# Hand-written engine programs with staging freed by each cast, a GpSimd relay of casts to TensorE's loop, and PSUM copies of four banks

## Chip, cores and metric

One Trainium2 chip, one core. The metric is the device time of one execution in microseconds (us). One run is one execution. "Span" is the time from the first to the last instruction of the profiled execution; the device time is 1.7 to 2.2 us longer.

Some terms. A semaphore is a counter on which an engine can wait. Each transfer adds 16 to its semaphore, in the transfers over 128 partitions one for each of the 16 DMA engines as it finishes its share; the last of the 16 is the landing. The *lag* below is the time from the median to the last of these increments, so how far the slowest DMA engine is behind. PSUM is the memory into which TensorE writes its sums; a group of two banks is 128x1024 float32 here. The granted clock is the share of its full clock that TensorE was given.

## The reference

```python
batch, m, k, n = 16, 512, 768, 1024
x: (16, 768, 512) float32      y: (16, 768, 1024) float32
out = np.einsum('bkm,bkn->bmn', x, y)          # (16, 512, 1024) float32
```

Each batch reads 1.57 MB of x and 3.15 MB of y and writes 2.10 MB. All 16 batches make 109.05 MB, and the kernel before and after move exactly these bytes.

## The kernel before

Four engine programs in one block. SyncE loads x and y into two staging buffers each, and stores. VectorE casts to bf16. TensorE runs 96 matmuls per loop round (two batches), 8 rounds. ScalarE copies PSUM to one of five output buffers, two banks at a time.

```python
LAG = 4; NO = 5                                    # stores lag 4 batches; 5 output buffers
# (cut: allocation of xs, ys, xb, yb (2 each), ob (5), ps (4 groups of 2 banks), semaphores)
@block.sync
def _(sync):
    def store(b):
        sync.wait_ge(outs, b + 1)
        sync.dma_start(o_v[b], ob[b % NO][:]).then_inc(so[b % NO], 16)
    for b in range(B):
        i = b % 2
        if b >= 2:
            sync.wait_ge(cast, b - 1)              # all casts of batch b-2
        sync.dma_start(xs[i][:], x_v[b]).then_inc(sx[i], 16)
        sync.dma_start(ys[i][:], y_v[b]).then_inc(sy[i], 16)
        if b >= LAG:
            store(b - LAG)
    for b in range(B - LAG, B):
        store(b)
    # (cut: wait for all stores)

@block.vector
def _(vector):
    for b in range(B):
        # (cut: i, ks; wait for TensorE's batch b-2, for x)
        nc.vector.tensor_copy(xb[i][:], xs[i][:]).then_inc(ready, 1)
        # (cut: wait for y)
        for h in range(2):                         # y in two halves of K
            nc.vector.tensor_copy(yb[i][:, ks], ys[i][:, ks]).then_inc(ready, 1)
        vector.drain().then_inc(cast, 1)

@block.scalar
def _(scalar):
    nc.scalar.nop().then_inc(room, MT)
    for b in range(B):
        for mo in range(MT):                       # 4 groups of 2 banks
            # (cut: waits for the output buffer and for TensorE's group)
            nc.scalar.copy(ob[b % NO][:, mo]..., ps[mo][:]).then_inc(room, 1)
        scalar.drain().then_inc(outs, 1)
```

Of the kernel before, what the change touches and what calls it, by code (L numbers as in the profile page):

```python
# [1 line left out]

_os.environ.setdefault("NEURON_RT_ULTRASERVER_MODE", "4")

# [1 line left out]

# [4 lines left out]


@with_exitstack
def kernel(
    ctx: ExitStack,
    tc: tile.TileContext,
    x: bass.AP,
    y: bass.AP,
    out: bass.AP,
):  # L20
    nc = tc.nc
    P = 128
    FP32 = mybir.dt.float32
    BF16 = mybir.dt.bfloat16

    B, K, M = x.shape
    _, _, N = y.shape
    KT = K // P
    MT = M // P
    NF = 512  # L30
    NT = N // NF



    x_v = x.rearrange("b (p ko) m -> b p ko m", ko=KT)
    y_v = y.rearrange("b (p ko) n -> b p ko n", ko=KT)
    o_v = out.rearrange("b (p mo) n -> b p mo n", mo=MT)

    LAG = 4
    NO = 5  # L40
    KH = KT // 2
    GP = NT * NF

    ctx.enter_context(tc.tile_critical())  # L44
    ec = ctx.enter_context
    xs = [ec(nc.sbuf_tensor(f"xs{i}", [P, KT, M], FP32)) for i in range(2)]
    ys = [ec(nc.sbuf_tensor(f"ys{i}", [P, KT, N], FP32)) for i in range(2)]
    xb = [ec(nc.sbuf_tensor(f"xb{i}", [P, KT, M], BF16)) for i in range(2)]
    yb = [ec(nc.sbuf_tensor(f"yb{i}", [P, KT, N], BF16)) for i in range(2)]
    ob = [ec(nc.sbuf_tensor(f"ob{i}", [P, MT, N], FP32)) for i in range(NO)]  # L50
    ps = [ec(nc.psum_tensor(f"ps{i}", [P, NT, NF], FP32)) for i in range(MT)]
    sx = [ec(nc.semaphore(f"sx{i}")) for i in range(2)]
    sy = [ec(nc.semaphore(f"sy{i}")) for i in range(2)]
    so = [ec(nc.semaphore(f"so{i}")) for i in range(NO)]
    cast = ec(nc.semaphore("cast"))
    ready = ec(nc.semaphore("ready"))
    room = ec(nc.semaphore("room"))
    groups = ec(nc.semaphore("groups"))
    outs = ec(nc.semaphore("outs"))
    block = ec(nc.Block())  # L60

    @block.sync
    def _(sync):
        def store(b):
            sync.wait_ge(outs, b + 1)
            sync.dma_start(o_v[b], ob[b % NO][:]).then_inc(so[b % NO], 16)

        for b in range(B):
            i = b % 2
            if b >= 2:  # L70
                sync.wait_ge(cast, b - 1)
            sync.dma_start(xs[i][:], x_v[b]).then_inc(sx[i], 16)
            sync.dma_start(ys[i][:], y_v[b]).then_inc(sy[i], 16)
            if b >= LAG:
                store(b - LAG)
        for b in range(B - LAG, B):
            store(b)
        for i in range(NO):
            sync.wait_ge(so[i], 16 * len(range(i, B, NO)))

    @block.vector
    def _(vector):
        for b in range(B):
            i = b % 2
            n = 16 * (b // 2 + 1)
            if b >= 2:
                vector.wait_ge(groups, MT * (b - 1))
            vector.wait_ge(sx[i], n)
            nc.vector.tensor_copy(xb[i][:], xs[i][:]).then_inc(ready, 1)  # L89
            vector.wait_ge(sy[i], n)  # L90
            for h in range(2):
                ks = slice(h * KH, (h + 1) * KH)
                nc.vector.tensor_copy(yb[i][:, ks], ys[i][:, ks]).then_inc(ready, 1)  # L93
            vector.drain().then_inc(cast, 1)

    def batch(tensor, i, first):
        x_w = xb[i][:].rearrange("p k (j mo) -> p k mo j", mo=MT)
        tensor.wait_ge(ready, 2).then_inc(ready, -2)
        for mo in range(MT):
            tensor.wait_ge(room, 1).then_inc(room, -1)  # L100
            for nt in range(NT):
                for kt in range(KT):
                    if mo == 0 and nt == 0 and kt == KH:
                        tensor.wait_ge(ready, 1).then_inc(ready, -1)
                    mm = nc.tensor.matmul(  # L105
                        ps[mo][:, nt], x_w[:, kt, mo],
                        yb[i][:, kt, nt * NF:(nt + 1) * NF],
                        start=(kt == 0), stop=(kt == KT - 1))
            mm.then_inc(groups, 1)

    @block.tensor
    def _(tensor):
        with tensor.Fori(0, B // 2):
            batch(tensor, 0, False)
            batch(tensor, 1, False)

    @block.scalar
    def _(scalar):
        nc.scalar.nop().then_inc(room, MT)
        for b in range(B):  # L120
            for mo in range(MT):
                if mo == 0 and b >= NO:
                    scalar.wait_ge(so[b % NO], 16 * (b // NO))
                scalar.wait_ge(groups, MT * b + mo + 1)
                nc.scalar.copy(ob[b % NO][:, mo].rearrange("p (t f) -> p t f", f=NF),  # L125
                               ps[mo][:]).then_inc(room, 1)
            scalar.drain().then_inc(outs, 1)


# [1 line left out]
_INS = ['x', 'y']  # L131
_OUTS = [((16, 512, 1024), 'float32')]


# [23 lines left out]
```

## Time and profile before

| | before |
|---|---|
| device time, median | 262.99 us (262.69 to 263.14, 3 runs) |
| span | 261.2 us |
| data queue, share of 16 DMA engines | 98.1% |
| TensorE, VectorE, ScalarE busy | 72%, 32%, 25% |
| last copy out of PSUM ends / store 15 issued / last byte confirmed | 250.72 / 250.78 / 259.79 us |

The first question to such a table is which row leaves no room. No compute engine does; the transfers do. The second question is whether that holds at the very end, because there a store has to wait for the last copy. The lines are in the prediction.

### The profile page before, as it was taken

What the parts mean: (1) busy time and instruction counts of PE and PEld (TensorE: products, weight loads), DVE (VectorE), ACT (ScalarE), POOL (GpSimd) and SP (SyncE); (2) the same over time, 40 slices, a digit from 0 to 9 for tenths busy, and PEclk for the clock granted to TensorE, in tenths of its full rate; (3) what the DMA queues carried; (4) which work ended last, traced back from release to release, by engine and by line L of the source; (5) the groups of instructions that cost most, each with busy time, mean ns of one, the idle gap of its engine ahead of it and who ended that gap; (6) DMA issues with size and microseconds to landing.
All of it is one profiled execution on the core that took longest, in us unless ns stands there. A gap on an engine that the chain in (4) does not pass through costs nothing. (4 is left out here: it accounts for less than half of the span.)

```text
span 261.2 us, 1938 instructions
## 1 busy us (share of the span) xinstructions
PE 188.0 (72%) x768; PEld 87.1 (33%) x768; DVE 83.0 (32%) x48; ACT 66.1 (25%) x65; POOL 0.2 (0%) x4
## 2 busy tenths in 40 slices
PE   0039999998948949398595997939678394896920
PEld 0014555443513515144152342514334142342500
DVE  0261734435223252322524214252132523225000
ACT  1003343433331314114032140412314033131410
POOL 0000000000000000000000000000000000000000
PEclk9999999999986999979798697997999899797995
DMA  7999999999999999999999999999999999999993
GB/s 265 431 425 427 438 411 453 425 386 418 446 420 439 420 430 446 415 441 420 439 437 412 447 423 440 415 432 442 423 434 420 435 433 423 440 433 421 434 421 141
DMA packets 6915, 109.09 MB, mean 418 GB/s; under 512 B 768, under 2 KB 768, under 8 KB 768
## 3 DMA queue, kind: packets, MB, share of 16 engines
q1 hardware_dynamic: 6912, 109.05, 98.1%
q8 instruction: 1, 0.02, 0.0%
q14 instruction: 2, 0.02, 0.0%
HBM read 75.50 MB, written 33.55 MB: 417 GB/s over the span
## 5 line engine op out<-in xcount | busy, mean ns | idle before, releaser
L105 PE MATMUL ps<-yb,xb 128*128 128x512 bf16 x768 | 188.0, 406 | 61.6 <-PEq L100 55.9
L105 PEld LDWEIGHTS ps<-yb,xb 128*128 128x128 bf16 x768 | 87.1, 116 | 162.1 <-issue 96.7
L125 ACT COPY ob<-ps 128x1024 f32<-128x1024 f32 x64 | 64.9, 1013 | 183.6 <-PE ps L105 183.6
L93 DVE CAST yb<-ys 128x3072 bf16<-128x3072 f32 x32 | 54.9, 1757 | 88.4 <-DMA ys<-in_y_dram 88.4
L89 DVE CAST xb<-xs 128x3072 bf16<-128x3072 f32 x16 | 28.2, 1760 | 67.5 <-DMA xs<-in_x_dram 66.8
L125 ACT ACT_TABLE_LOAD x1 | 1.3, 1283 | 1.0 <-SPq L44 1.0
L142 POOL MEMSET const-uint8-127<- 128x1 uint8 x1 | 0.1, 102 | 0.0
L142 POOL MEMSET const-bfloat16-1.0<- 128x1 bf16 x1 | 0.1, 101 | 0.0
L142 POOL MEMSET const-float32-0.0<- 128x1 f32 x1 | 0.1, 98 | 0.2 <-issue 0.2
L142 POOL MEMSET const-float32-1.0<- 128x1 f32 x1 | 0.1, 98 | 0.0
## 6 DMA issues: line engine op xcount, KB each, us to landing
ys<-in_y_dram SPq DMA_DIRECT2D x16, 3072.0 KB, 27.7
out_dram<-ob SPq DMA_DIRECT2D x16, 2048.0 KB, 32.1
xs<-in_x_dram SPq DMA_DIRECT2D x16, 1536.0 KB, 20.8
```

The costliest lines, as they stand in the source:

```text
L89: nc.vector.tensor_copy(xb[i][:], xs[i][:]).then_inc(ready, 1)
L93: nc.vector.tensor_copy(yb[i][:, ks], ys[i][:, ks]).then_inc(ready, 1)
L105: mm = nc.tensor.matmul(ps[mo][:, nt], x_w[:, kt, mo], yb[i][:, kt, nt * NF:(nt + 1) * NF], start=(kt == 0), stop=(kt == KT - 1))
L125: nc.scalar.copy(ob[b % NO][:, mo].rearrange("p (t f) -> p t f", f=NF), ps[mo][:]).then_inc(room, 1)
L142: nc = _bacc.Bacc("TRN2", target_bir_lowering=False, num_devices=1)
```

## The change

Its intent: issue each load as soon as its own staging buffer is free, halve the ScalarE instructions, cast y in one instruction where TensorE has time, let stores 0 to 13 wait for TensorE's next batch, and drop the block with its entry and exit. VectorE now counts all casts in one semaphore `cast`; GpSimd waits on fixed values of it and feeds `ready`, which TensorE's loop decrements.

```diff
-    ps = [... [P, NT, NF] ... for i in range(MT)]          # 4 groups of 2 banks
+    ps = [... [P, HB, NT, NF] ... for i in range(2)]       # 2 groups of 4 banks
-    block = ec(nc.Block())                                 # (all programs now stand without it)
+    def parts(b):
+        return 2 if b in (0, 1, 2, 14, 15) else 1
     def store(b):
-            sync.wait_ge(outs, b + 1)
+        if b < B - 2:
+            nc.sync.wait_ge(groups, 2 * (b + 2))            # TensorE's batch b+1 done
+        else:
+            nc.sync.wait_ge(outs, b - (B - 3))
     for b in range(B):
         if b >= 2:
-                sync.wait_ge(cast, b - 1)
+            nc.sync.wait_ge(cast, nx[b - 2])                # x cast of b-2
         dma_start(xs[i][:], x_v[b])
+        if b >= 2:
+            nc.sync.wait_ge(cast, nx[b - 2] + parts(b - 2)) # last y cast of b-2
         dma_start(ys[i][:], y_v[b])
-            for h in range(2):                              # y cast in halves, then a drain
+        for h in range(parts(b)):                           # one y cast in batches 3 to 13
+    for b in range(B):
+        nc.gpsimd.wait_ge(cast, nx[b]).then_inc(ready, 1)
+        for h in range(parts(b)):
+            nc.gpsimd.wait_ge(cast, nx[b] + h + 1).then_inc(ready, 2 // parts(b))
     # ScalarE: 2 copies of 128x2048 per batch instead of 4 of 128x1024; drain only in batch 14
     # (cut: TensorE's loop, same 96 matmuls, now room/groups per 4 banks)
```

More of the change, by code (lines that the diff above doesn't have):

```diff
@@ L10 @@
 from concourse._compat import with_exitstack
+from concourse.ordered_engine_set import OrderedEngineSet
 @with_exitstack
@@ L41 @@
     KH = KT // 2
-    GP = NT * NF
     ctx.enter_context(tc.tile_critical())
@@ L50 @@
     ob = [ec(nc.sbuf_tensor(f"ob{i}", [P, MT, N], FP32)) for i in range(NO)]
-    ps = [ec(nc.psum_tensor(f"ps{i}", [P, NT, NF], FP32)) for i in range(MT)]
+    HB = MT // 2
+    ps = [ec(nc.psum_tensor(f"ps{i}", [P, HB, NT, NF], FP32)) for i in range(2)]
     sx = [ec(nc.semaphore(f"sx{i}")) for i in range(2)]
@@ L59 @@
     outs = ec(nc.semaphore("outs"))
-    block = ec(nc.Block())
-    @block.sync
-    def _(sync):
-        def store(b):
-            sync.wait_ge(outs, b + 1)
-            sync.dma_start(o_v[b], ob[b % NO][:]).then_inc(so[b % NO], 16)
-        for b in range(B):
-            i = b % 2
-            if b >= 2:
-                sync.wait_ge(cast, b - 1)
-            sync.dma_start(xs[i][:], x_v[b]).then_inc(sx[i], 16)
-            sync.dma_start(ys[i][:], y_v[b]).then_inc(sy[i], 16)
-            if b >= LAG:
-                store(b - LAG)
-        for b in range(B - LAG, B):
-            store(b)
-        for i in range(NO):
-            sync.wait_ge(so[i], 16 * len(range(i, B, NO)))
@@ L81, in _ @@
-    @block.vector
-    def _(vector):
-        for b in range(B):
-            i = b % 2
-            n = 16 * (b // 2 + 1)
-            if b >= 2:
-                vector.wait_ge(groups, MT * (b - 1))
-            vector.wait_ge(sx[i], n)
-            nc.vector.tensor_copy(xb[i][:], xs[i][:]).then_inc(ready, 1)
-            vector.wait_ge(sy[i], n)
-            for h in range(2):
-                ks = slice(h * KH, (h + 1) * KH)
-                nc.vector.tensor_copy(yb[i][:, ks], ys[i][:, ks]).then_inc(ready, 1)
-            vector.drain().then_inc(cast, 1)
@@ L96, in batch @@
-    def batch(tensor, i, first):
-        x_w = xb[i][:].rearrange("p k (j mo) -> p k mo j", mo=MT)
-        tensor.wait_ge(ready, 2).then_inc(ready, -2)
-        for mo in range(MT):
-            tensor.wait_ge(room, 1).then_inc(room, -1)
-            for nt in range(NT):
-                for kt in range(KT):
-                    if mo == 0 and nt == 0 and kt == KH:
-                        tensor.wait_ge(ready, 1).then_inc(ready, -1)
-                    mm = nc.tensor.matmul(
-                        ps[mo][:, nt], x_w[:, kt, mo],
-                        yb[i][:, kt, nt * NF:(nt + 1) * NF],
-                        start=(kt == 0), stop=(kt == KT - 1))
-            mm.then_inc(groups, 1)
@@ L111, in _ @@
-    @block.tensor
-    def _(tensor):
-        with tensor.Fori(0, B // 2):
-            batch(tensor, 0, False)
-            batch(tensor, 1, False)
-    @block.scalar
-    def _(scalar):
-        nc.scalar.nop().then_inc(room, MT)
-        for b in range(B):
-            for mo in range(MT):
-                if mo == 0 and b >= NO:
-                    scalar.wait_ge(so[b % NO], 16 * (b // NO))
-                scalar.wait_ge(groups, MT * b + mo + 1)
-                nc.scalar.copy(ob[b % NO][:, mo].rearrange("p (t f) -> p t f", f=NF),
-                               ps[mo][:]).then_inc(room, 1)
-            scalar.drain().then_inc(outs, 1)
+    def parts(b):
+        return 2 if b in (0, 1, 2, 14, 15) else 1
@@ new lines, with store @@
+    nx = [sum(1 + parts(a) for a in range(b)) + 1 for b in range(B)]
+    def store(b):
+        if b < B - 2:
+            nc.sync.wait_ge(groups, 2 * (b + 2))
+        else:
+            nc.sync.wait_ge(outs, b - (B - 3))
+        nc.sync.dma_start(o_v[b], ob[b % NO][:]).then_inc(so[b % NO], 16)
+    for b in range(B):
+        i = b % 2
+        if b >= 2:
+            nc.sync.wait_ge(cast, nx[b - 2])
+        nc.sync.dma_start(xs[i][:], x_v[b]).then_inc(sx[i], 16)
+        if b >= 2:
+            nc.sync.wait_ge(cast, nx[b - 2] + parts(b - 2))
+        nc.sync.dma_start(ys[i][:], y_v[b]).then_inc(sy[i], 16)
+        if b >= LAG:
+            store(b - LAG)
@@ new lines @@
+    for b in range(B - LAG, B):
+        store(b)
+    for b in range(B):
+        i = b % 2
+        n = 16 * (b // 2 + 1)
+        if b >= 2:
+            nc.vector.wait_ge(groups, 2 * (b - 1))
+        nc.vector.wait_ge(sx[i], n)
+        nc.vector.tensor_copy(xb[i][:], xs[i][:]).then_inc(cast, 1)
+        nc.vector.wait_ge(sy[i], n)
+        for h in range(parts(b)):
+            ks = slice(h * KT // parts(b), (h + 1) * KT // parts(b))
+            nc.vector.tensor_copy(yb[i][:, ks], ys[i][:, ks]).then_inc(cast, 1)
@@ new lines, with batch @@
+    for b in range(B):
+        nc.gpsimd.wait_ge(cast, nx[b]).then_inc(ready, 1)
+        for h in range(parts(b)):
+            nc.gpsimd.wait_ge(cast, nx[b] + h + 1).then_inc(ready, 2 // parts(b))
+    def batch(i):
+        x_w = xb[i][:].rearrange("p k (j mo) -> p k mo j", mo=MT)
+        nc.tensor.wait_ge(ready, 2).then_inc(ready, -2)
+        for g in range(2):
+            nc.tensor.wait_ge(room, 1).then_inc(room, -1)
+            for m in range(HB):
+                for nt in range(NT):
+                    for kt in range(KT):
+                        if g == 0 and m == 0 and nt == 0 and kt == KH:
+                            nc.tensor.wait_ge(ready, 1).then_inc(ready, -1)
+                        mm = nc.tensor.matmul(
+                            ps[g][:, m, nt], x_w[:, kt, g * HB + m],
+                            yb[i][:, kt, nt * NF:(nt + 1) * NF],
+                            start=(kt == 0), stop=(kt == KT - 1))
+            mm.then_inc(groups, 1)
@@ new lines @@
+    pe = nc.tensor.engine
+    with nc.Fori(0, B // 2, engines=OrderedEngineSet([pe])):
+        batch(0)
+        batch(1)
+    nc.scalar.nop().then_inc(room, 2)
+    for b in range(B):
+        if b >= NO:
+            nc.scalar.wait_ge(so[b % NO], 16 * (b // NO))
+        for g in range(2):
+            nc.scalar.wait_ge(groups, 2 * b + g + 1)
+            cp = nc.scalar.copy(ob[b % NO][:, g * HB:(g + 1) * HB].rearrange("p m (t f) -> p m t f", f=NF),
+                                ps[g][:])
+            if b < B - 1:
+                cp.then_inc(room, 1)
+        if b == B - 2:
+            nc.scalar.drain().then_inc(outs, 1)
@@ L131 @@
+    cp.then_inc(outs, 1)
+    for i in range(NO):
+        nc.sync.wait_ge(so[i], 16 * len(range(i, B, NO)))
 _INS = ['x', 'y']
```

## The prediction

> **What bounds the kernel now.** I read the page first: per-engine busy shares, the 40 slices, the DMA queue.
>
> ```profile
> PE 188.0 (72%) x768; PEld 87.1 (33%) x768; DVE 83.0 (32%) x48; ACT 66.1 (25%) x65; POOL 0.2 (0%) x4
> ...
> DMA  7999999999999999999999999999999999999993
> ...
> q1 hardware_dynamic: 6912, 109.05, 98.1%
> ...
> q8 instruction: 1, 0.02, 0.0%
> ```
>
> No compute engine is busy more than 72% of the span, but the DMA row is full from the second slice to the last but one, and the data queue fills 98.1% of 16 engines for the whole span. So the transfers are the bound. Before I believe that, I ask whether they are full everywhere, or starve at the two ends. The windows view of the same run answers (columns: window, length, busy time and count of PE, PEld, DVE, ACT, POOL, then granted clock, DMA share, GB/s):
>
> ```profile
> 4.00:20.00 16.00, 2.88 (x7) 0.88 (x8) 6.51 (x4) 0.00 (x0) 0.00 (x0) 1.00 1.02 435
> 20.00:100.00 80.00, 69.41 (x303) 33.86 (x301) 29.82 (x18) 25.33 (x25) 0.00 (x0) 0.96 1.01 428
> 100.00:220.00 120.00, 91.41 (x365) 41.39 (x363) 38.35 (x23) 31.42 (x31) 0.00 (x0) 0.90 1.00 430
> 220.00:250.00 30.00, 24.35 (x96) 10.95 (x96) 8.35 (x5) 7.38 (x8) 0.00 (x0) 0.89 1.01 430
> ...
> 251.00:251.50 0.50, 0.00 (x0) 0.00 (x0) 0.00 (x0) 0.00 (x0) 0.00 (x0) 1.00 0.54 229
> 251.50:252.50 1.00, 0.00 (x0) 0.00 (x0) 0.00 (x0) 0.00 (x0) 0.00 (x0) 1.00 1.04 442
> ...
> 256.50:257.00 0.50, 0.00 (x0) 0.00 (x0) 0.00 (x0) 0.00 (x0) 0.00 (x0) 0.50 0.24 98
> ...
> 258.00:258.50 0.50, 0.00 (x0) 0.00 (x0) 0.00 (x0) 0.00 (x0) 0.00 (x0) 0.50 0.15 66
> 258.50:259.00 0.50, 0.00 (x0) 0.00 (x0) 0.00 (x0) 0.00 (x0) 0.00 (x0) 0.50 0.08 33
> ```
>
> From 4 to 250 us the DMA moves 428 to 435 GB/s without a gap, whichever of the other engines is busy. There is one dip, to 0.54 for half a microsecond around 251.25, and a ragged end: at 258.5 only 0.08 x 16, about one engine, still works. The dip is the wait for the last store. The chain of waits shows what leads to it:
>
> ```profile
> 239.14 10.54 PE ps L105 x45
> 249.69 0.02 issue
> 249.71 1.01 ACT ob L125
> ```
>
> The last copy out of PSUM ends at 250.72 and store 15 is issued at 250.78 (timeline of the DMA issues). It looks as if compute set the end. It nearly does, but not quite: the trace's completion records give 16 increments per transfer, one for each DMA engine. For store 14 they come at 251.55 (first), 252.36 (median), 254.21 (fifteenth) and 254.96 (last); for store 15 at 256.89, 257.18, 259.05 and 259.79. The last engine needs 259.79 - 254.96 = 4.83 us for its eighth packet after the previous set; its eight packets of 16 KB take about 0.61 us each (611 ns median), 4.9 us. So the slowest engine went from store 14 to store 15 without a pause. Only the earliest engines ran dry for some tenths of a microsecond, and they don't set the end. The run ends with the slowest DMA engine's own bytes, then 261.2 - 259.8 = 1.4 us of barriers.
>
> **What the Trainium skill says.** "DMA: Bandwidth & Descriptors", section "Where 436 GB/s comes from", puts the ceiling of the 16 ports at 435.2 GB/s; this trace agrees with 428 to 435 in every long window, so 1.5% or less is left there. The same page, "Why a DMA increments its semaphore by 16 and not by 1", says the engines finish independently and each posts its own +1 after its data; the trace agrees (median to last 0.75 us at the first load, 2.62 us at the last store: the lag grows). "ScalarE: Activation LUTs", section "What ACT_TABLE_LOAD costs", gives 186 ns + 0.833 ns per element with immediate operands; the trace's copy of 1024 elements takes 1013 ns, where that gives 1039, so slope right and fixed part nearer 160. "Runtime: NRT & Kernel Launch", section "Instruction fetch mechanics", says a sequencer refills its instruction memory in 16 KiB blocks by DMA; the trace has one such packet of 16,384 bytes at 38.0 us, and between the landings of 36.97 and 41.86 us the slowest engine's lag rises from 0.77 to 1.98 us. So what an instruction fetch costs here is about 1.2 us on one DMA engine.
>
> **The change part by part.** The bytes, the 48 transfers and their order in the one queue (x, y, store, x, y, store) stay; the order comparison of the built kernels shows the same sequence on SyncE. So the sum below starts from the same transfer time.
>
> 1. Staging freed by each cast: x of batch b is issued after the x cast of b-2 instead of after its y cast. In the trace the loads are issued with a y load and a store still queued (y takes 27.7 us from issue to landing, of which its own 3.1 MB at 430 GB/s are 7.3). An earlier place in a queue that never empties is worth 0.
> 2. y casts merged in batches 3 to 13 (parts = 1): TensorE starts after one cast of 6144 columns, estimated from 1757 ns for 3072 (slope about 0.52 ns, fixed 157 ns) as 3.36 us, instead of after the first half: 1.6 us later per batch. TensorE's work per batch is 188.0 / 16 = 11.75 us, against a period of 15.8 us between loads of y, so 4.0 us of slack less the later start's 1.6 still leaves it keeping pace. Off the path: 0.
> 3. GpSimd hands on the casts: one more semaphore hop. In the trace a barrier hop through GpSimd (its release to the other engines' wake) is 0.04 to 0.1 us; I take 0.1 to 0.2 us at each TensorE start. The last batch feels it, the others don't.
> 4. ScalarE copies four banks at once: 32 copies of 2048 elements, estimated as 160 + 853 x 2 = 1.87 us each. Total 60 us instead of 64.9: irrelevant. But the last copy is 0.86 us longer, behind the same last matmul.
> 5. Store 15 is therefore issued about 0.86 + 0.15, so 1.0 us later: 251.8. First packets follow an issue by about 1.0 us (0.94 to 1.95 at the start). At 252.8 the slowest engine is still on store 14: its increment of 254.96, less the 0.4 us that increments land after they run, makes 254.6. So 1.8 us of slack remain. The fast engines wait one microsecond more and end at about 257.7 + 0.4. Worth at the end: 0.
> 6. Stores b < 14 wait for TensorE's batch b+1 instead of for the copies. Store b is issued at loop step b+4, after y of b+2 is cast, 15.8 + 3.4 us after y of b+1 landed; TensorE's batch b+1 is done about 3.8 + 12 us after that landing. Margin 3 us: 0. Store 13 now waits for batch 14 (done near 235 us), with stores 11 and 12 still queued, which takes it to 242: 0.
> 7. The block with its own entry branch and exit barrier goes. In the trace the exit barrier runs from 259.80 to 260.18: 0.37 us, after the last byte, so all of it counts. The entry branch before the first load is 0.05 to 0.1 us. Together -0.4 us.
>
> Sum: 263.0 - 0.4 = 262.6 us.
>
> **The rivals.** (a) *Compute takes over the end.* The chain ends in TensorE and ScalarE, and the dip to 0.54 shows store 15 is almost late; the change makes it 1.0 us later. If the slowest engine's lag of 2.6 us were under 0.8 us, this would set the end. But then the whole run would end sooner, at 251.8 + 1.0 + 4.9 + 0.4 = 258.1 instead of 259.8: that rival makes 261.0. (b) *The lag moves.* Instruction fetches depend on program length and place; DVE, ACT and TensorE get shorter, GpSimd longer. One fetch more or fewer on the slowest engine is about 0.6 to 1.2 us: 261.4 to 263.8. For it to be large, TensorE's loop would have to refetch each of its 8 rounds; the kernel before, with the same loop body, shows one fetch in all, so I give this 2% (+5 to 10 us). (c) *The queue runs dry.* If the later TensorE start and the stricter store waits stalled SyncE by more than the queue's content (x and y of one batch, 4.7 MB, 11 us), there would be gaps in each period. The margin of 3 us and those 11 us speak against it; it would make 265 to 275. (d) *The freed staging really raises throughput.* At 430 of 435 GB/s the most it could win is 1.2% of 253 us, 3 us: 260. Nothing in the windows speaks for it: rate is the same with more or fewer transfers queued.
>
> **Range and chances.** Before scatters over 0.45 us in three runs. With (b) as the main spread, 8 times in 10 between 261.5 and 263.6. Over 2% faster means under 257.7 us, so 109.05 MB in some 252 us including the ramp of 1 us: the rate would have to pass the ceiling nearly. 1%. Slower by over 2% (268.3) needs (c) or the refetch: 2%.
>
> **What the profile of after would show.** DMA row full again, data queue near 98%, long windows at 428 to 435 GB/s; the copies of 128x2048 at 1.87 us and casts of 128x6144 at 3.36; SyncE's waits moved from the cast after y to both casts; TensorE's starts 1.6 us later in batches 3 to 13 only; store 15 issued about 1 us later with a deeper dip before it; last increment near 259.7 and 1.0 us, not 1.4, behind it. I am wrong if the DMA row has holes in the middle, if store 15's last engine starts it late, or if instruction packets multiply.

## The result

| | before | after |
|---|---|---|
| device time, median | 263.06 us (262.69 to 263.26, 4 runs) | 262.92 us (262.82 to 263.13, 4 runs) |
| span of the profiled run | 261.2 | 260.8 |
| store 15 issued | 250.78 | 250.75 |
| last byte confirmed | 259.79 | 259.54 |
| from there to the end of the span | 1.44 | 1.23 |

The ratio is 0.9997, 95% interval 0.998 to 1.0014: the same time. Ratios here are the mean time of one kernel's runs over that of the other's of the same rounds, so not quite the ratio of the quoted medians. Executions over 1.5% slower than the fastest of the same kernel are left out of the means.

The page of the kernel after, the rows that answer to those of before:

```profile
PE 188.0 (72%) x760; PEld 88.9 (34%) x768; DVE 82.2 (32%) x37; ACT 61.1 (23%) x33; POOL 0.2 (0%) x4
...
DMA  6999999999999999999999999999999999999993
...
q1 hardware_dynamic: 6912, 109.05, 98.1%
q8 instruction: 1, 0.02, 0.0%
```

The instruction counts fell (VectorE 48 to 37, ScalarE 65 to 33); the DMA row and the queue's share stand where they stood. (The 760 matmuls are 768 with eight records missing; the weight loads show all.) The windows of the kernel after, columns as in the prediction (a packet counts in the window in which it starts, so a share can pass 1):

```profile
4.00:20.00 16.00, 3.41 (x8) 1.03 (x9) 6.95 (x4) 0.00 (x0) 0.00 (x0) 1.00 1.01 435
20.00:100.00 80.00, 67.43 (x287) 33.17 (x289) 29.10 (x13) 22.43 (x12) 0.00 (x0) 0.94 1.01 428
100.00:220.00 120.00, 94.32 (x373) 43.90 (x375) 38.10 (x16) 29.88 (x16) 0.00 (x0) 0.89 1.00 430
220.00:250.00 30.00, 22.79 (x95) 10.82 (x96) 8.11 (x5) 6.75 (x4) 0.00 (x0) 0.94 1.01 432
...
251.00:251.50 0.50, 0.00 (x0) 0.00 (x0) 0.00 (x0) 0.00 (x0) 0.00 (x0) 1.00 0.62 262
```

435, 428, 430 and 432 GB/s stand against 435, 428, 430 and 430 before. The chain of waits of the kernel after still ends in TensorE and ScalarE:

```profile
238.95 9.89 PE ps L124 x45
248.84 0.02 issue
248.86 1.86 ACT ob L142
```

The last copy is 0.85 us longer than before, yet it ends at the same time, because the matmuls ahead of it took 9.89 us instead of 10.54 and started 0.2 us earlier. The granted clock was different; the windows over the start of the last batch, first before, then after (the number after the fifth pair of brackets is the granted TensorE clock):

```profile
237.60:241.00 3.40, 3.30 (x9) 1.10 (x10) 1.40 (x1) 0.00 (x0) 0.00 (x0) 0.57 0.97 414
```

```profile
237.40:241.00 3.60, 2.81 (x12) 1.42 (x14) 1.35 (x1) 0.00 (x0) 0.00 (x0) 1.00 1.02 437
```

In the trace of before, TensorE was granted 0.57 of its clock there; after, all of it. I take this for chance and not for a merit of the change: in late_x below, whose last batch has the same instructions, the clock was 0.71 over 5 us of it. With the matmuls of before, store 15 would have come some 0.6 us later (an estimate from 10.54 - 9.89); whether that matters is what the first experiments ask.

The costliest groups by shape, kernel after: the new instructions have the durations that the prediction estimated (1.87 and 3.36 us). For the cast it split one duration, 1757 ns, into a slope and a fixed part, which one form alone cannot give; the two forms measured now do, 0.52 ns a column and 152 ns.

```profile
L142 ACT COPY ob<-ps 128x2048 f32<-128x2048 f32 x32 | 59.8, 1868 | 188.7 <-PE ps L124 188.7
L105 DVE CAST yb<-ys 128x6144 bf16<-128x6144 f32 x11 | 37.0, 3360 | 61.5 <-DMA ys<-in_y_dram 61.5
```

### The profile page after: what moved, and what is told of

Read it like the earlier page. It is cut to its first block, busy times and chain, and to the rows that moved or that the text cites. A ratio compares the mean times of both kernels' runs of the same rounds, so it can differ in the third digit from the quotient of the medians.

```text
span 260.8 us, 1850 instructions
## 1 busy us (share of the span) xinstructions
PE 188.0 (72%) x760; PEld 88.9 (34%) x768; DVE 82.2 (32%) x37; ACT 61.1 (23%) x33; POOL 0.2 (0%) x4
## 5 line engine op out<-in xcount | busy, mean ns | idle before, releaser
L124 PEld LDWEIGHTS ps<-yb,xb 128*128 128x128 bf16 x768 | 88.9, 118 | 159.4 <-issue 93.9
L142 ACT COPY ob<-ps 128x2048 f32<-128x2048 f32 x32 | 59.8, 1868 | 188.7 <-PE ps L124 188.7
L105 DVE CAST yb<-ys 128x6144 bf16<-128x6144 f32 (+1 forms) x21 | 54.1, 2596 | 88.5 <-DMA ys<-in_y_dram 88.5
## 6 DMA issues: line engine op xcount, KB each, us to landing
xs<-in_x_dram SPq DMA_DIRECT2D x16, 1536.0 KB, 29.7
```

Source lines behind the costliest of these rows:

```text
L105: nc.vector.tensor_copy(yb[i][:, ks], ys[i][:, ks]).then_inc(cast, 1)
L124: mm = nc.tensor.matmul(ps[g][:, m, nt], x_w[:, kt, g * HB + m], yb[i][:, kt, nt * NF:(nt + 1) * NF], start=(kt == 0), stop=(kt == KT - 1))
L142: cp = nc.scalar.copy(ob[b % NO][:, g * HB:(g + 1) * HB].rearrange("p m (t f) -> p m t f", f=NF), ps[g][:])
```

## The experiments

Theory A: the transfers are the bound everywhere; a part of the change is worth only what it alters in the DMA engines' work or after their last byte. Rival B: the chain of TensorE and ScalarE sets the end. Rival C: parts of the change are worth something each and cancel.

### Nothing but the transfers (dma_only)

```diff
-    (all casts, GpSimd's relay, the matmuls, the PSUM copies)
+    for i in range(NO):
+        nc.vector.memset(ob[i][:], 0.0).then_inc(outs, 1)
     # loads of batch b: wait for the landing of the load of b-2 into the same buffer
     # stores: same place in the queue, wait only for the clearing
```

> Wrong result on purpose (the output is zeros): the 48 transfers of the changed kernel in the same order, with no cast, no matmul and no PSUM copy; VectorE clears the five output buffers once, loads wait for the landing of the load two before, stores for the clearing. Theory A (the transfers are the bound): 261.3 to 263.0 us, although TensorE and ScalarE do nothing; at the lower end if the 16 KB instruction packet near 37 us, which should then be gone, is what puts the slowest engine behind. Rival B (the chain of TensorE and ScalarE at the end, 4.5% of the span in the changed kernel, is what the time waits for): 252 us or less.

Measured: 262.51 us median (262.05 to 263.34, 6 runs), ratio to before 0.998 (0.9966 to 0.9994); the result is wrong, as intended. From its page:

```profile
DVE 17.4 (7%) x5; POOL 0.2 (0%) x4
...
DMA  7999999999999999999999999999999999999993
...
q1 hardware_dynamic: 6912, 109.05, 98.1%
```

With no matmul in the program the time falls by 0.2%. This is what the transfers cost by themselves, in this order and from this queue, and it shows A: nothing that the change does to the compute engines could have won more than about 0.5 us (0.9 at the lower end of the interval). B's 252 us is refuted.

It also took down a reading of mine. There is no instruction packet in this run, so the rise of the slowest engine's lag at 37 us is gone. But the lag grows all the same, in steps at other times: median to last increment 0.27 us at 51 us, 0.76 at 84, 1.42 at 140, 1.98 at 156, 2.62 at 212, 2.64 at the end (kernel after: 2.53). In every trace with that packet the lag rises by 1.2 to 1.6 us between two landings around it (0.77 to 1.98 before, 0.17 to 1.68 after), and here it does not (0.28 to 0.27): the fetch brings the lag early, but at the end it is as large without one.

### Undoing the earlier x loads (late_x)

```diff
-            nc.sync.wait_ge(cast, nx[b - 2])
+            nc.sync.wait_ge(cast, nx[b - 2] + parts(b - 2))
         nc.sync.dma_start(xs[i][:], x_v[b]).then_inc(sx[i], 16)
```

> The changed kernel with one part undone: x of a batch is issued after the y cast of the batch two before, as in the kernel before. Theory A (the transfers are the bound and the queue never empties, so an earlier place in it is worth nothing): 262.9 us, within 0.3 us of the changed kernel, long windows at 428 to 435 GB/s, x takes about 21 us from issue to landing instead of 29.7. Rival C (the parts cancel: earlier staging wins about 0.5 us or more, which something else gives back): 263.4 us or more.

Measured: 262.87 us median (262.63 to 262.87, 5 runs). The median time from issue to landing of x falls from 29.7 us to 20.9, and the landings don't move (median difference 0.04 us): x waits 8.8 us longer in the queue when issued 8.8 us earlier. A holds; C falls for this part. A gift of chance: in this trace the clock was granted at 0.71 from 240 to 245 us, and store 15 was issued at 252.38, 1.6 us later than in the kernel after. The span is 260.7 against 260.8.

### Delaying the last store (copy_x2, copy_x5)

```diff
-            cp = nc.scalar.copy(...)
+            for r in range(2 if b == B - 1 and g == 1 else 1):    # 5 in copy_x5
+                if r:
+                    nc.scalar.drain()
+                cp = nc.scalar.copy(...)
```

> The changed kernel with the very last PSUM copy done twice (same data, a drain between), so store 15 is issued about 2.0 us later. Theory A (the slowest DMA engine is still on store 14; its data of store 14 ends near 254.3, while store 15 issued at 250.75 could start at 251.7, so there are 1.8 to 2.65 us of slack, depending on the granted clock in the last batch): 262.9 us, at most 0.3 more. Rival B (TensorE and ScalarE set the end, as the chain of waits shows it): +2.0, 264.9 us.

> The changed kernel with the very last PSUM copy done five times, so store 15 is issued about 8.0 us later, beyond the slack. Theory A: 8.0 less the slack of 1.8 to 2.65, so +5.3 to +6.2: 268.2 to 269.1 us. Rival B: +8.0, 270.9 us. If the time does not move at all, both are wrong.

Measured: 263.96 us median (262.87 to 264.39, 4 runs) and 269.46 us (268.95 to 270.32, 4 runs). The ends of the three timelines, late_x, copy_x2 and copy_x5 (start, duration, instruction):

```profile
250.49 1.87 ACT L142 COPY ob<-ps 128x2048 f32<-128x2048 f32 x1 [3.26 <-PE ps L124]
252.38 0.33 SPq L79 DMA_DIRECT2D out_dram<-ob  x1
```

```profile
251.05 3.80 ACT L145 COPY ob<-ps 128x2048 f32<-128x2048 f32 x2 [3.26 <-PE ps L124]
254.88 0.33 SPq L79 DMA_DIRECT2D out_dram<-ob  x1
```

```profile
250.09 9.59 ACT L145 COPY ob<-ps 128x2048 f32<-128x2048 f32 x5 [3.25 <-PE ps L124]
259.71 0.33 SPq L79 DMA_DIRECT2D out_dram<-ob  x1
```

Set each profiled run's issue of store 15 against its end:

| run | store 15 issued | span | span less issue |
|---|---|---|---|
| after | 250.75 | 260.8 | 10.0 |
| banks2 (below) | 251.62 | 260.8 | 9.2 |
| late_x | 252.38 | 260.7 | 8.3 |
| copy_x2 | 254.88 | 262.4 | 7.5 |
| copy_x5 | 259.71 | 267.2 | 7.5 |

Up to 252.4 the span does not answer at all; past some point it follows one to one, 7.5 us behind. The two lines meet at 260.8 - 7.5, so at an issue of 253.3, and the kernel after has 2.5 us of slack. This is the slowest engine's lag seen from the other side: as long as one engine still works on store 14, store 15 may be late for the other fifteen. The increments of late_x show it: fifteen come from 258.49 to 258.63, some 6.2 us after the issue, and the last at 259.49, where the kernel after has 259.54; in copy_x2 all 16 come within 0.15 us, 6.1 to 6.3 us after the issue. My expectation for copy_x2 (at most 0.3 us) was missed: in its profiled run the last matmul ended 2.2 us later than in the kernel after, so the issue passed the limit by 1.6 us. The scatter of its four runs, 1.5 us, fits an issue that falls on either side of the limit, but only one of them has a trace. The median of copy_x5, 6.5 us above the kernel after, also lies a little over what I expected (5.3 to 6.2); the issue moved by 9.0 us in its traced run, not by 8.0, and the span by 6.4.

### Two banks per copy, and the last store in halves (banks2, split15)

```diff
# banks2: HB = 1, ps in 4 groups of 2 banks, waits on groups and room scaled to 4 per batch
# split15:
+        if b == B - 1:
+            nc.sync.dma_start(o_v[b][:, :HB], ob[b % NO][:, :HB]).then_inc(so[b % NO], 16)
+            nc.sync.wait_ge(outs, 3)
+            nc.sync.dma_start(o_v[b][:, HB:], ob[b % NO][:, HB:]).then_inc(so[b % NO], 16)
```

> The changed kernel with the PSUM part undone: four groups of two banks, 64 copies of 128x1024, as before. Theory A: store 15 is issued about 0.86 us sooner for the same clock in the last batch, and the time stays within 0.3 us of 262.9. Rival B: 262.0 us.

> The changed kernel with store 15 in two halves, the first issued after the first of the two last PSUM copies, about 5 us earlier, the second after the last copy. The fast engines should then not run dry near 251. Theory A (the slowest engine never ran dry): 262.9 us, within 0.3. Rival B (the end hangs on the last store's issue): half the bytes are left at the same issue, 2.4 us less, 260.5 us.

Measured: banks2 262.93 us (262.84 to 263.15, 4 runs), although its traced run issued store 15 at 251.62, not sooner: its last matmul ended later than in the kernel after; split15 262.9 us (262.67 to 263.15, 5 runs). In split15 the first half went out at 247.97 us and the second at 253.09; half the bytes were left at a later issue than in any uncut version above that kept its time, and the end did not move either way (last increment 259.59 against 259.54). Both are as A has it, and neither the larger copies nor their undoing is visible in the time. Of C, then, two parts are refuted one by one (x loads, copies); the others were not undone singly, and dma_only alone limits what they could win.

### How much queue is enough (late_all, one_deep)

```diff
# late_all: both loads of b wait until TensorE has finished b-2
-            nc.sync.wait_ge(cast, nx[b - 2])
+            nc.sync.wait_ge(groups, 2 * (b - 1))
# one_deep: both loads of b wait for the last y cast of b-1
-            nc.sync.wait_ge(cast, nx[b - 2])
+            nc.sync.wait_ge(cast, nx[b - 1] + parts(b - 1))
```

> The changed kernel, but the loads of a batch are issued only when TensorE has finished the batch two before, about 12 us later than in the changed kernel (y cast end to TensorE end), near the landing of the y before. Theory A (a queue with a store of 4.9 us still in it hides this; only an empty queue costs): 262.9 to 264.5 us, the data queue at 97 to 98%. Rival C (earlier issue of loads is a gain of its own): each of 14 batches loses something like 1 us or more, 277 us or more.

> The changed kernel, but the loads of a batch wait for the y cast of the batch just before, so at each issue only one store is queued: new data can start 4.4 us after a landing of y on the slowest engine (cast 3.4, issue to first packet 1.0), while the store queued there lasts 4.9 us and on the median engine, 2.5 us ahead, runs out some 2.4 us too early. Theory A: the slowest engine just stays fed once the stores flow (batch 4 on), the first three loads without a store lose up to 4.4 us each and are the only gaps on it: 272 to 280 us, with dips in every period on the fast engines. If depth of the queue did not matter at all: 262.9.

Measured: late_all 280.83 us (279.6 to 282.62, 3 runs; a fourth, 287.06, was slow), one_deep 314.22 us (312.28 to 316.87, 4 runs). Both are far above what I expected, and by the number alone late_all is where C was to be (277 or more). Its windows show that the loss is not spread over the batches as C has it:

```profile
20.00:30.00 10.00, 9.95 (x45) 5.05 (x44) 3.43 (x2) 2.42 (x2) 0.00 (x0) 1.00 0.43 184
...
50.00:62.00 12.00, 11.95 (x52) 6.04 (x52) 3.36 (x1) 3.74 (x2) 0.00 (x0) 0.93 0.37 144
...
100.00:200.00 100.00, 71.84 (x289) 33.74 (x291) 31.53 (x13) 22.75 (x13) 0.00 (x0) 0.90 1.01 424
```

The DMA stands still where no store is in the queue yet: 10 x (1 - 0.43) + 12 x (1 - 0.37) = 13.3 us of the 19.8 by which this run's span exceeds that of the kernel after are in these two windows. Once stores flow, the DMA has no gaps, as A said. What I forgot was the start. The other 6 us are load packets that take longer: y takes the mean engine 121.6 us instead of 117.7, x 61.7 instead of 59.5. A did not foresee that. In one_deep there are more gaps and more slow packets (windows of that run):

```profile
20.00:30.00 10.00, 9.95 (x46) 5.23 (x46) 3.43 (x2) 2.84 (x2) 0.00 (x0) 1.00 0.49 199
30.00:50.00 20.00, 13.34 (x54) 5.87 (x53) 5.19 (x3) 4.63 (x3) 0.00 (x0) 0.85 0.64 255
50.00:66.00 16.00, 10.47 (x43) 4.96 (x43) 5.12 (x2) 3.74 (x2) 0.00 (x0) 0.82 0.68 280
...
100.00:200.00 100.00, 63.78 (x241) 29.05 (x245) 27.15 (x11) 18.68 (x10) 0.00 (x0) 0.81 0.92 350
```

Up to 66 us the DMA stands still for 5.1 + 7.2 + 5.1 = 17.4 us. From 100 us on the share stays at 0.92 while the rate falls to 350 GB/s: the engines count as busy and move less. The packets of the y loads take longer, a tenth of them over 1.55 us where the kernel after has 0.92, and the mean engine spends 133.6 us on them instead of 117.7 (x: 68.2 instead of 59.5; stores 78.3 in both). So of the 54 us by which this run's span is longer, 15.9 + 8.7 = 24.6 are slower load packets, and the rest is standing still. Why a load's packets slow down when little is queued is not settled by these runs; slow y packets also appear in the kernel before, in the kernel after and in dma_only, nearly all in one group near 55 us. Both runs show that the depth of the queue is worth a lot, but that before and after are both on the safe side of it: x issued 8.8 us later, as in before, cost nothing in late_x.

### More instruction fetches (unroll)

```diff
-    with nc.Fori(0, B // 2, engines=OrderedEngineSet([pe])):
+    for _ in range(B // 2):
         batch(0)
         batch(1)
```

> The changed kernel with TensorE's loop written out, 8 times the code, about 1536 matmul and weight-load instructions[...]. If the 16 KB instruction packet at 37.7 us is TensorE's, there will be 6 to 12 such packets, and if they run on the slowest DMA engine (its lag rose from 0.16 to 1.5 us with that packet), its lag grows by 1.2 to 1.5 us with each: 270 to 280 us. If they are spread over engines or on another engine: below 265 us. If the packet is not TensorE's: one packet, 262.9 us.

Measured: 262.96 us (262.8 to 263.3, 4 runs), ratio to before 1.0004 (0.9987 to 1.002). The trace has six 16 KB instruction packets, at 37, 71, 118, 151, 198 and 229 us, so they are TensorE's. But the lag of the slowest engine stays at 2.4 us from 70 us on, and is 2.1 at the end. The five further packets cost nothing that the time shows. The trace doesn't name the DMA engine of a packet, but the landings tell enough: with each of the five, one y packet takes 1.38 to 1.46 us instead of 0.91, and after each, one more engine posts its increment over 1.75 us behind the first, one after the second packet and five after the sixth, while the slowest stays 3.2 to 3.4 us behind. So they fell on engines that had time to spare, the second of the three cases that I had set out. (My text misread the first packet's effect in the kernel after: the lag rose from 0.17 to 1.68 us, not from 0.16 to 1.5.)

### One engine less in the last store (tail15)

```diff
+        if b == B - 1:
+            nc.sync.dma_start(o_v[b][:120], ob[b % NO][:120]).then_inc(so[b % NO], 16)
+            nc.sync.dma_start(o_v[b][120:], ob[b % NO][120:]).then_inc(so[b % NO], 16)
```

> The changed kernel with store 15 split in two: 120 partitions, which divide over 15 DMA engines, and 8 partitions over 8. If the one slowest engine is the sixteenth, it has nothing to do after store 14 (last increment 254.7) and the others end near 257.5 to 258.1, plus 0.6 for one packet more on eight of them: the last increment falls from 259.5 to about 258, and the time to 261.0 to 261.8 us. If the slowest engine is another one, nothing is won and up to 0.6 us lost: 262.9 to 263.5. Rival B expects no change in either case.

Measured: 268.24 us (267.91 to 269.02, 5 runs), ratio to before 1.0212 (1.0198 to 1.0226). Neither of the two outcomes came. The windows of this run:

```profile
254.00:256.00 2.00, 0.00 (x0) 0.00 (x0) 0.00 (x0) 0.00 (x0) 0.00 (x0) 0.67 0.84 197
256.00:258.00 2.00, 0.00 (x0) 0.00 (x0) 0.00 (x0) 0.00 (x0) 0.00 (x0) 0.50 1.01 254
```

The engines are busy, at half the rate. The median 16 KB packet that starts after 252.6 us takes 1.21 us, a quarter of them 1.27 or more, where stores over 128 partitions show 0.61. The split trades one late engine for many slow packets. Why they are slow, and which engine is the late one, can't be read from it.

## Why the prediction was right

It said 262.6 us (261.5 to 263.6) and 97% for the same time; measured were 262.92 us. By its own steps:

1. *Earlier x loads, worth 0.* Shown by late_x.
2. *One y cast in batches 3 to 13, TensorE 1.6 us later, worth 0.* From the start of the y cast to the first matmul 2.06 us became 3.71 in those batches, so 1.65. TensorE kept pace, with 1.9 to 5.3 us idle before each of them (before, 0.4 to 4.5). That this costs nothing in the time was not tested alone; dma_only limits all compute steps together to about 0.5 us.
3. *GpSimd's hop, 0.1 to 0.2 us.* Too large: from the end of the first y cast to the first matmul 0.30 us became 0.35 in the last batch and similar batches, so 0.05.
4. *Copies of 1.87 us.* 1868 ns.
5. *Store 15 issued 1.0 us later, harmless within 1.8 us of slack.* The step from the last matmul to the issue rose by 0.82 us (1.09 to 1.91), and the hop ahead of it by 0.05, so 0.9 of the 1.0. The issue itself did not move, because the clock granted in the last batch differed and y of batch 15 landed 0.25 us earlier. The latest harmless issue that the prediction implies, 251.8 + 1.8 = 253.6, is 253.3 by the delays above. That the issue stayed 2.5 us short of it and not 1.8 is luck with the clock. The conclusion stands without it: late_x was 1.6 us later at no cost.
6. *Stricter store waits, worth 0.* The long windows have no dip, and the last store that waits for TensorE's batch went out at 234.5 us with others still queued.
7. *No block, -0.4 us.* This is the mis-sized term: first load issued at 0.937 us against 0.938, so the entry is worth nothing; the time behind the last byte fell from 1.44 to 1.23 us, so -0.2. The prediction took the whole stretch of 259.80 to 260.18 for the barrier, but about 0.15 us of it are SyncE's own steps after the last store wait, which stay.

With -0.2 in place of -0.4 the sum is 262.8. In the nine other traces of variants of the change (all but dma_only, which waits for more at its end) the time behind the last byte is 1.22 to 1.23 us too; for before there is one trace. The difference of 0.14 us between the medians is smaller than the scatter of either, so no runs show even that much as a gain; the traces show the 0.2 us.

Of the rivals, (a), compute takes over the end, is refuted by dma_only, and its limit is measured: 2.5 us. (b), the lag moves with instruction fetches, did not come: six fetches or none leave the lag at the end between 2.1 and 2.7 us. What a second fetch on the slowest engine would do, no run shows. (c) was a real danger of another design, as one_deep shows, not of this one. (d) would have needed a higher rate, and there was none. (The room above 428 GB/s is 1.7% of 435.2, not "1.5% or less"; nothing rests on it.)

No version here beats the two kernels, and dma_only says how little there is to beat with these transfers: 0.2%.

## What to carry to other kernels

When one resource is full from the second slice to the last but one, build the kernel that has only this resource's work; what it saves is the most that any change elsewhere can win, and a few runs tell. A chain of waits that ends in compute does not prove that compute sets the end: see which of the parallel DMA engines finishes last and whether it ever waited, or delay the suspected step and see from which delay on the time follows. And issue loads early enough for the phase in which nothing else is queued, the start, where a late issue is not hidden (13.3 us in late_all).

## What the Trainium skill lacked or had wrong

- "DMA: Bandwidth & Descriptors", "Where 436 GB/s comes from", from which the prediction takes the ceiling of 435.2 GB/s, also says that transfers between HBM and SBUF are bound by HBM at about 358 GB/s, half of a stack's 716. Here, with one core at work, such transfers moved 428 to 435 GB/s in every long window.
- The same page, "Why a DMA increments its semaphore by 16 and not by 1", has 120 partitions divided over 15 engines (the largest divisor up to 16), and does not say that this can be slower. In tail15, the median 16 KB packet took 1.21 us instead of 0.61, and the time rose by 2.1%.
- The same page has the engines finish independently, but no figure for how far they drift. In a queue that is never empty the slowest ran 2.1 to 2.7 us behind the median at the end, and this hid a last store up to 2.5 us late.
- No page has load packets slow down in a shallow queue: in one_deep a tenth of the 24 KB packets took over 1.55 us, in the kernel after over 0.92.
- "ScalarE: Activation LUTs", "What ACT_TABLE_LOAD costs", gives an ACTIVATE with immediate operands a fixed 186 ns; the copies of 1013 ns (1024 elements) and 1868 ns (2048), which the trace calls COPY, give 0.835 ns per element and 158 ns fixed.
- "Runtime: NRT & Kernel Launch", "Instruction fetch mechanics", calls the cost of crossing a block mostly hidden, and five more TensorE blocks indeed changed the time by a ratio of 1.0004 (0.9987 to 1.002). It does not say that a block's packet holds up a data-moving DMA engine, here by 1.2 to 1.6 us (the rise of the lag at 37 us).
